# Two mixer layers on one core: a share of the second output projection moves into the attention before it, and four smaller moves

## The chip, the cores and the metric

One Trainium2 chip, one of its cores. The time is device microseconds of one execution: 2440.41 us median of 3 runs (2439.42 to 2441.58). TensorE (PE), VectorE (DVE), ScalarE (ACT), GpSimd (POOL) and SyncE (SP, which issues the transfers) each run their own instruction list in its order; an instruction that waits holds all that stand behind it on its engine.

## The reference

Two layers, run on 1024 latent and 256 context tokens. What matters of a layer:

```
h = rmsnorm(x) * (1 + scale) + shift          # scale, shift, gate from c and w_ada
u = h @ w_in                                   # q, k, v, gates, Hyena, RG-LRU
y_attn = softmax(q k^T / 8) v                  # 8 query heads on 2 key heads, 64 wide
y_hy   = Hyena, a long convolution by FFT;  y_lru = a recurrence in both directions
mix = [y_attn*silu(g_attn), y_hy*silu(g_hy), y_lru*silu(g_lru)]     # 1536 wide
x = x + gate * (mix @ w_out)
```

Latent queries see 512 cached, 1024 latent keys and none of the context; context queries see 256 keys. A last rmsnorm follows layer 2.

## The kernel before, in words

Features lie on partitions, the 1280 tokens along the free axis in chunks of 512, 512 and 256. Each fp32 matrix product is made of three fp16 products: an operand is split into a rounded part (`hi`) and a remainder (`lo = x - hi`), and hi*hi, hi*lo and lo*hi are added up in PSUM.

Stages, in time: **start** (loads; sums of squares of x; scale and shift from `w_ada`; `make_h`, L585), **layer 1**: input projection with recurrence, Hyena and filter spectra woven in (`weave` hands out steps of side generators at fixed rates), **attention 1**, **output projection 1** (with the second layer's filter and `w_ada` work woven in), then **layer 2** in the same way up to **output projection 2**, which runs alone, and the final rmsnorm.

At the start `Squares` squares each x tile on ScalarE and adds the squares up on GpSimd (chunks 1 and 3) or VectorE (chunk 2); TensorE then sums over partitions. Each tile is multiplied by the reciprocal root (half of the tiles on GpSimd), and `make_h` makes the rounded part on ScalarE, the scaled tile on VectorE and the remainder on GpSimd or VectorE. `small_params` (some 60 tiny VectorE operations) stands ahead of this in VectorE's list.

`attention` walks 40 units: 4 pairs of heads, 5 blocks of 256 queries, 2 heads. A unit of latent queries has 12 key tiles in 6 positions of two, one of context queries 1 position. `scores` makes per position 4 score matmuls (L1174, L1175) into one PSUM bank; ScalarE writes exp in fp32 to `by`; the rounded exp is made from the same scores on ScalarE again (`A`), or as a cast on VectorE (`V`) or GpSimd (`G`); the remainder is a subtraction on VectorE or GpSimd. The table `SPLIT` names both engines for each position. `values` multiplies the unit before by v (48 matmuls, L1200 and L1201), VectorE normalises, and after the second head `emit_out` transposes (L1212), gates and splits the result. Between units, row maxima of the next pair are made (`q_maxima`: 48 matmuls of 512 columns, each followed by a VectorE reduction, L1149 and L1150), in bursts of three.

`outproj` (L1291) makes for each of 8 output tiles and 3 chunks 36 matmuls: 12 inputs by three products. Inputs 4 to 11 (Hyena, recurrence) were parked in HBM (`Md`) and are loaded back to `h` tiles; inputs 0 to 3 come from the attention. PSUM is shared by tag: `acc` 3 banks, `s` 2, `m` 2, `o` 1. A scheduler sets each engine's list from the program's order and its estimates.

Of the kernel before, what the change touches and what calls it, by code (L numbers as in the profile page):

```python
# [55 lines left out]
BUFS = {"h": 8, "f": 4, "a": 8, "y": 8, "by": 6, "ld": 4, "bn": 4, "ba": 2, "wr": 4, "wh": 10, "acc": 2, "s": 2, "o": 2, "m": 2}  # L56
# [6 lines left out]
R_FM = (2.006, 1.505)  # L63
# [9 lines left out]
EARLY = (11, 0)  # L73
PTAG = {"acc": "acc", "nacc": 3, "s": "s", "ns": 2, "o": "o", "no": 1, "m": "m", "nm": 2}
BM, VEARLY = 1, True
ORD = "wwwwxwxwxwxwxwxwxwxwcwwww"
# [5 lines left out]
XE = "GVVG"  # L82
SE = "GVG"
# [11 lines left out]
HLO = ((3,), (0,))  # L95
WENG = {"l": "V", "h": "V", "k": "V", "v": "V", "q": "G", "g": "V", "o": "V"}

SPLIT = ("AG", "VV", "AG", "AV", "GG", "AG"), \
    ("VG", "VG", "VV", "VV", "VV", "AG")
# [13 lines left out]
def hybrid_step(ctx, tc, xT, cT, w_ada, w_in, w_out, prm, fpk, w1, w2, w3, decay, ck, cv, wlru,  # L113
# [35 lines left out]
    def stt(out, a, s, b, o0=MUL, o1=ADD, eng=None):  # L149
        (eng or V).scalar_tensor_tensor(out, a, s, b, o0, o1)  # L150
# [44 lines left out]
    Xs = dr.tile([KT, P, T], F32, name="Xs")  # L195
    Qd = dr.tile([2, 2, 2, P, T], F16, name="Qd")
# [264 lines left out]
    def ada():  # L461

        sc = cp.tile([P, KT, 2], F32, name="silu_c")
        th = sm.tile([P, KT, 2], F32, name="th_c")
        act(th, cT_t, AF.Tanh, scale=0.5)
        V.tensor_scalar(th, th, 0.5, 0.5, MUL, ADD)
        tt(sc, th, cT_t, MUL)
        for o in (0, 8):
            p = [PS("s" if o else "acc") for _ in range(2)]
# [78 lines left out]
    class Squares:  # L548
# [17 lines left out]
        def rstd_all(self, chunks):  # L566
            p, t = {}, {}
            for tag, (c0, n) in zip(("m", "m", "acc"), chunks):
                p[c0] = PS(tag)[:, :n]
                PE.matmul(p[c0], ones, self.at(c0, n), start=True, stop=True)  # L570
            for c0, n in chunks:
                t[c0] = rstd_start(p[c0], D)
            for c0, n in chunks:
                rstd_newton(self.at(c0, n), p[c0], D, t[c0])
                yield c0, n, self.at(c0, n)

# [6 lines left out]

    def h_tiles():
        return [S("h", (P, 2, W5), F16) for _ in range(KT)]  # L585

    def make_h(l, h, xs, c0, n):

        s = 0 if c0 < NL else 1
        for i in range(KT):  # L590
            x = xs[i][:, c0:c0 + n]
            hi, lo = h[i][:, 0, c0:c0 + n], h[i][:, 1, c0:c0 + n]
            if l == 0:
                act(hi, x, AF.Identity, scale=sc_t[:, l, i, s:s + 1], bias=sh_t[:, l, i, s:s + 1])
                V.tensor_scalar(x, x, sc_t[:, l, i, s:s + 1], sh_t[:, l, i, s:s + 1], MUL, ADD)
            else:
                act(hi, x, AF.Copy)
            tt(lo, x, hi, SUB, V if i % 4 in HLO[l] else G)

# [15 lines left out]
    class Weights:  # L615


        def __init__(self):
            self.todo, self.done, self.live = [], {}, []
            for l in range(DEPTH):  # L620
                hy = lambda i: [f"hy{n}{i}" for n in (2, 1, 0, 3)]
                names = [f"l{x}{i}" for i in range(4) for x in ("x", "g")]
                names = [n.replace("lg", "gl") for n in names]
                names += hy(0) + hy(1) + ["k", "v", "qa0", "qb0"] + hy(2) + hy(3) + ["qa1", "qb1"]
                names += [f"ga{i}" for i in range(4)] + list(range(KT))
                self.todo += [(l, n) for n in names]
            self.cap = BUFS["wh"]

        def pull(self, need=None):
            while self.todo:  # L630
                l, n = self.todo[0]
                size = 3 if isinstance(n, int) else 2
                if need not in self.done and need is not None:
                    pass
                elif sum(x[1] for x in self.live) + size > self.cap:
                    break
                self.todo.pop(0)
                self.live.append(((l, n), size))
                if isinstance(n, int):
                    v = [split_w(w_out[l, n, :, 512 * i:512 * i + 512], WENG["o"]) for i in (1, 2, 0)]  # L640
                else:
                    v = [split_w(w_in[l, TIDX[n], :, 512 * i:512 * i + 512], WENG[n[0]]) for i in range(2)]
                self.done[l, n] = v
# [487 lines left out]
    def q_maxima(pair, q, tag="m"):  # L1131

        q["q"] = q_head(pair)
        mxl = sm.tile([P, 16, 3], F32, tag="mxl", name=nm("mxl"))
        m = sm.tile([P, 20], F32, tag="mm", name=nm("mm"))
        for i in range(20):
            q_max((*q["q"], mxl, m), i, tag)
            yield
        q["mt"] = q_finish(mxl, m)
        yield  # L1140

    def q_max(st, i, tag="m"):
# [3 lines left out]
        if qt < 8:  # L1146
            for c in range(3):
                p = PS(tag)
                PE.matmul(p, lhs, k1[g][:, 512 * c:512 * c + 512], start=True, stop=True)  # L1149
                V.tensor_reduce(mxl[:, 8 * e + qt, c:c + 1], p, AX.X, MAX)  # L1150
        else:
# [3 lines left out]
            V.tensor_reduce(m[:, o:o + 1], p[:, :NP], AX.X, MAX)  # L1155

# [8 lines left out]
    def scores(st, e, c0, last):  # L1165
# [4 lines left out]
        for s2 in range(0, ns, 2):  # L1170
# [12 lines left out]
            how = SPLIT[last][s2 // 2]  # L1183
# [6 lines left out]
            tt(pt[:, 1, k:k + 2], x, hi, SUB, V if how[1] == "V" else G)  # L1190
        return pts
# [45 lines left out]
    def attention(l, h, st, gates, fill, every):  # L1237
        units = [(p, c0, e) for p in range(4) for c0 in range(0, T, 256) for e in range(2)]
        prev, mix, done = None, [], 0
# [7 lines left out]
        mx, steps = maxima(), 21 * (4 - FM[l])  # L1247
        for n, (pair, c0, e) in enumerate(units):
            k = n % 10
# [4 lines left out]
            if pair < 3:  # L1254
                while done < -(-steps * (n + 1) // 30):
                    next(mx, None)
                    done += 1
                if n == 29:
                    drain(mx)
            pts = scores(st[pair], e, c0, pair == 3)  # L1260
# [7 lines left out]
        drain(fill)  # L1268
        values(*prev[0])
        emit_out(prev[0][4], gates[3], prev[0][2], mix)  # L1270
        return mix

    def outproj(l, mix, xn, sq, rs, ahead):

        for ds in [(d,) for d in range(KT - LAST)] + [tuple(range(KT - LAST, KT))]:
# [4 lines left out]
            for c0, n in CH:  # L1280
                for d in ds:
                    w = W.get(l, d)
                    xi = B("ba")
                    load(xi[:, :n], (xT if l == 0 else Xs)[d, :, c0:c0 + n])
                    acc = PS("acc")
                    for ki in range(NMIX):
                        k = (ki + 4) % NMIX
                        hi, lo = w[ki // 4]
                        cs = slice(P * (k % 4), P * (k % 4) + P)
                        for j, (wt, x) in enumerate(((hi, 0), (hi, 1), (lo, 0))):  # L1290
                            PE.matmul(acc[:, :n], wt[:, cs], mix[k][:, x, c0:c0 + n],  # L1291
                                      start=(ki == 0 and j == 0), stop=(ki == NMIX - 1 and j == 2))
                    if c0 == NL:
                        W.free(l, d)
                    s = 0 if c0 < NL else 1
                    x = xo[d][:, c0:c0 + n]
                    stt(x, acc[:, :n], gt_t[:, l, d, s:s + 1], xi[:, :n])
# [51 lines left out]
    sq, rs = Squares(), {}  # L1349
    for i in range(KT):  # L1350
        for c0, n in CH:
            sq.add(i, xs[i][:, c0:c0 + n], c0, n, ENG[SE[c0 // 512]])
# [7 lines left out]
    for c0, n, r in sq.rstd_all(CH):  # L1360
        for i in range(KT):
            x = xs[i][:, c0:c0 + n]
            tt(x, x, r, MUL, ENG[XE[i % 4]])
    W.pull()
    for l in range(DEPTH):
        h = h_tiles()

        def prep(c0, n):
            if l and c0:
                through(l - 1, c0, n, xs, rs[c0])  # L1370
            make_h(l, h, xs, c0, n)
            if l == 0 and c0 == 0:
                keep_hidden(hid)
            if l == 0 and c0 == NL:
                small_params()
# [36 lines left out]
        mix = attention(l, h, st, gates, fill, EVERY[l])  # L1412
        for i in range(8):
            m = S("h", (P, 2, W5), F16)
            load(m[:, :, :T], Md[i])
            mix.append(m)
# [159 lines left out]
```

## Time and profile before

| | us |
|---|---|
| median of 3 runs | 2440.41 |
| profiled execution | 2441.38 |
| its span, first to last instruction | 2439.6 |
| PE busy | 2123.0 (87%) |
| DVE busy | 1883.6 (77%) |
| ACT busy | 1182.0 (48%) |
| POOL busy | 885.8 (36%) |

The span is the time of the profiled execution but for 1.8 us around it. Busy shares are averages over stages with different limits, so the stages are read one by one. Matmuls are pipelined, and the profile counts each to its own end: a busy PE is not yet a full one.

### The profile page before, as it was taken

What the parts mean: (1) busy time and instruction counts of PE and PEld (TensorE: products, weight loads), DVE (VectorE), ACT (ScalarE), POOL (GpSimd) and SP (SyncE); (2) the same over time, 40 slices, a digit from 0 to 9 for tenths busy, and PEclk for the clock granted to TensorE, in tenths of its full rate; (3) what the DMA queues carried; (4) which work ended last, traced back from release to release, by engine and by line L of the source; (5) the groups of instructions that cost most, each with busy time, mean ns of one, the idle gap of its engine ahead of it and who ended that gap; (6) DMA issues with size and microseconds to landing.
All of it is one profiled execution on the core that took longest, in us unless ns stands there. A gap on an engine that the chain in (4) does not pass through costs nothing. (4 is left out here: it accounts for less than half of the span.)

```text
span 2439.6 us, 37801 instructions
## 1 busy us (share of the span) xinstructions
PE 2123.0 (87%) x14270; PEld 1254.3 (51%) x14270; DVE 1883.6 (77%) x2946; ACT 1182.0 (48%) x2026; POOL 885.8 (36%) x803
## 2 busy tenths in 40 slices
PE   7488878989998878879999898998899888887997
PEld 1144444555455556665445444555555556666554
DVE  7888798387678899986867878747756999998324
ACT  5476655344333556644353676633433346674211
POOL 6732251134213466852111311122341247785100
PEclk8699989999999999979999999999999999998999
DMA  6324215133124400004554122223421431000113
GB/s 260 92 57 123 70 50 134 57 121 123 65 64 151 154 22 7 1 2 125 174 178 149 54 44 42 49 78 114 127 85 60 122 126 54 4 5 1 59 51 108
DMA packets 140871, 205.11 MB, mean 84 GB/s; under 512 B 20612, under 2 KB 68909, under 8 KB 140688
## 3 DMA queue, kind: packets, MB, share of 16 engines
q1 hardware_dynamic: 140688, 202.69, 27.4%
q8 instruction: 112, 1.84, 0.3%
q14 instruction: 71, 0.58, 0.1%
HBM read 160.25 MB, written 38.54 MB: 81 GB/s over the span
## 5 line engine op out<-in xcount | busy, mean ns | idle before, releaser
L659 PE MATMUL acc<-h,wh 128*128 128x512 f16 (+1 forms) x3264 | 861.3, 351 | 48.2 <-ACT h L156 22.4
L659 PE MATMUL acc<-h,wl 128*128 128x512 f16 (+1 forms) x1632 | 572.3, 351 | 0.0
L659 PEld LDWEIGHTS <-wh 128*128 128x128 f16 x3264 | 324.0, 99 | 324.6 <-issue 80.3
L153 POOL TENSOR_TENSOR y<-by,y 128x512 f16<-128x512 f32 x256 | 326.5, 1293 | 147.9 <-ACT y L156 81.7
L659 PEld LDWEIGHTS <-wl 128*128 128x128 f16 x1632 | 162.2, 99 | 156.7 <-issue 29.7
L156 ACT ACTIVATE f<-acc 128x512 f32<-128x512 f32 (+1 forms) x204 | 105.4, 519 | 252.5 <-PE acc L659 243.3
L156 ACT ACTIVATE by<-s 128x512 f32<-128x512 f32 x208 | 126.6, 609 | 160.1 <-PE s L1175 128.7
L1291 PE MATMUL acc<-h,wh 128*128 128x512 f16 (+1 forms) x768 | 202.4, 346 | 0.0
L1150 DVE TENSOR_REDUCE mxl<-m 128x1 f32<-128x512 f32 x288 | 189.0, 680 | 10.1 <-PE m L1149 9.9
L150 DVE SCALAR_TENSOR_TENSOR a<-f,pr,a 128x1024 f32<-128x1024 f32 (+1 forms) x144 | 145.0, 1026 | 59.7 <-ACT a L156 57.5
L1200 PE MATMUL o<-va,y 128*128 128x130 f16 x1600 | 168.3, 228 | 8.9 <-DVE ba L153 5.5
L153 DVE TENSOR_TENSOR y<-by,y 128x512 f16<-128x512 f32 x144 | 169.7, 1210 | 1.0
L1201 PE MATMUL o<-va,y 128*128 128x65 f16 x1600 | 162.8, 199 | 3.8 <-DVE y L153 3.8
L1149 PE MATMUL m<-k,a 128*128 128x512 f16 x288 | 107.4, 395 | 64.3 <-DVE mxl L1150 58.6
L1200 PEld LDWEIGHTS <-y 128*128 128x128 f16 x1600 | 151.2, 102 | 19.9 <-DVE ba L153 8.2
L1291 PEld LDWEIGHTS <-wh 128*128 128x128 f16 x1152 | 111.4, 98 | 96.3 <-issue 14.6
L370 PE MATMUL m<-y,ld 128*128 128x256 f16 x960 | 128.6, 282 | 33.9 <-ACT y L156 14.1
L1201 PEld LDWEIGHTS <-y 128*128 128x128 f16 x1600 | 148.1, 101 | 12.4 <-issue 5.0
L150 DVE SCALAR_TENSOR_TENSOR wl<-wr,wh 128x512 f16<-128x512 f32 x168 | 133.2, 805 | 16.1 <-ACT wh L156 15.1
L156 ACT ACTIVATE wh<-wr 128x512 f16<-128x512 f32 x184 | 112.7, 623 | 59.5 <-PE acc L659 34.6
L153 DVE TENSOR_TENSOR y<-y,y 128x256 f32<-128x256 f32 (+4 forms) x160 | 131.2, 849 | 11.2 <-ACT y L156 11.1
L156 ACT ACTIVATE by<-acc 128x512 f32<-128x512 f32 x192 | 118.2, 615 | 32.4 <-PE acc L1175 25.6
(216 smaller groups left out, 4277.1 us busy)
## 6 DMA issues: line engine op xcount, KB each, us to landing
wr<-in_w_in SPq DMA_DIRECT2D x136, 256.0 KB
bn<-in_w_ada SPq DMA_DIRECT2D x64, 256.0 KB
wr<-in_w_out SPq DMA_DIRECT2D x48, 256.0 KB
ld<-in_fhl SPq DMA_DIRECT2D x56, 192.0 KB
h<-Md SPq DMA_DIRECT2D x16, 640.0 KB
h<-in_w_ada SPq DMA_DIRECT2D x16, 512.0 KB
Md<-ba SPq DMA_DIRECT2D x32, 256.0 KB
Hl<-by SPq DMA_DIRECT2D x32, 256.0 KB
```

Source lines behind the costliest of these rows:

```text
L150: (eng or V).scalar_tensor_tensor(out, a, s, b, o0, o1)
L153: (eng or V).tensor_tensor(out, a, b, op)
L156: A.activation(out, a, f, bias=bias, scale=scale)
L370: PE.matmul(x[:, o], cn[:, y, c], hl[:, z, g], start=(k == 0 and j == 0), stop=(k == 1 and j == 2))
L659: PE.matmul(acc[:, :n], w[k // 4][wi][:, P * (k % 4):P * (k % 4) + P], h[k][:, x, c0:c0 + n], start=(k == 0 and j == 0), stop=(k == KT - 1 ...
L1149: PE.matmul(p, lhs, k1[g][:, 512 * c:512 * c + 512], start=True, stop=True)
L1150: V.tensor_reduce(mxl[:, 8 * e + qt, c:c + 1], p, AX.X, MAX)
L1200: PE.matmul(o[:, qt], p[:, 0], va[g][:, s0 + s], start=(s == 0), stop=False)
L1201: PE.matmul(o[:, qt, 0], p[:, 1], va[g][:, s0 + s, 0], start=False, stop=(s == ns - 1))
L1291: PE.matmul(acc[:, :n], wt[:, cs], mix[k][:, x, c0:c0 + n], start=(ki == 0 and j == 0), stop=(ki == NMIX - 1 and j == 2))
```

## The change

It edits five places.

1. **Start.** `FirstSquares` adds the squares in pairs, and TensorE adds up the pairs over tiles and partitions in PSUM (12 fp32 matmuls in place of 3). The multiplication by the reciprocal root falls into one VectorE operation with the scale; the rounded part gets its shift on ScalarE. Constants load first, and `small_params` is queued behind the third chunk.
2. **Attention, both layers.** The maxima come one at a time after each position, not three at a time; `emit_out` runs one unit later. Rates of the same work ahead of the attention are rescaled to the finer steps.
3. **Attention 2 alone.** `SPLIT` gets a row for each layer: in layer 2 every rounded exp is ScalarE's, 4 of 6 remainders GpSimd's, 2 VectorE's.
4. **Output projection 2.** `soon` makes the products with inputs 4 to 11 inside attention 2, one (output tile, chunk) about every 1.4 units from the fifth on, adds x and stores the sum to HBM (`Xp`); `outproj` loads it and adds inputs 0 to 3.
5. The buffers `ba` grow from 2 to 3.

```diff
-BUFS = {..., "ba": 2, ...}
+BUFS = {..., "ba": 3, ...}
...
+SOON, SOON_RATE, SOON_FROM = (1,), 0.71, 4
-SPLIT = ("AG", "VV", "AG", "AV", "GG", "AG"), \
-    ("VG", "VG", "VV", "VV", "VV", "AG")
+SPLIT = (("AG", "VV", "AG", "AV", "GG", "AG"), ("VG", "VG", "VV", "VV", "VV", "AG")), \
+    (("AG", "AG", "AV", "AG", "AG", "AV"), ("AG", "AG", "AV", "AG", "AG", "AV"))
...
+    class FirstSquares:
+        def add(self, i, x, c0, n):
+            sq = B("bn" if i % 2 else "by")[:, :n]
+            act(sq, x, AF.Square)
+            if i % 2 == 0:
+                self.even[c0] = sq
+            else:
+                tt(sq, sq, self.even[c0], ADD, G if c0 == 512 else V)
+                PE.matmul(self.acc[c0][:, :n], ones, sq, start=(i == 1), stop=(i == KT - 1))
...
     def make_h(...)
-            if l == 0:
-                act(hi, x, AF.Identity, scale=sc_t[:, l, i, s:s + 1], bias=sh_t[:, l, i, s:s + 1])
-                V.tensor_scalar(x, x, sc_t[:, l, i, s:s + 1], sh_t[:, l, i, s:s + 1], MUL, ADD)
+            if r is not None:
+                sh = sh_t[:, l, i, s:s + 1]
+                done = stt(x, x, sc_t[:, l, i, s:s + 1], r, MUL, MUL)
+                act(hi, x, AF.Identity, bias=sh)
+                if i in HFIRST:
+                    stt(lo, x, sh, hi, ADD, SUB)
+                else:
+                    act(x, x, AF.Identity, bias=sh)
+                    tt(lo, x, hi, SUB, G)
...
     def attention(...)
+            if sooner and n >= SOON_FROM:
+                have += SOON_RATE
+                if have >= 1.0:
+                    have -= 1.0
+                    next(sooner, None)
...
                 values(*prev[0])
+                if late:
+                    emit_out(*late.pop())
                 if prev[0][1]:
-                    emit_out(prev[0][4], gates[prev[1]], prev[0][2], mix)
+                    late.append((prev[0][4], gates[prev[1]], prev[0][2], mix))
...
+    def soon(l, parked):
+        for d in range(KT):
+            w = W.get(l, f"u{d}")
+            for c0, n in CH:
+                xi = B("ld")[:, :n]
+                load(xi, (xT if l == 0 else Xs)[d, :, c0:c0 + n])
+                acc = out_acc(w, [None] * 4 + parked, range(4, NMIX), c0, n)
+                if c0 == NL:
+                    W.free(l, f"u{d}")
+                s = 0 if c0 < NL else 1
+                stt(xi, acc, gt_t[:, l, d, s:s + 1], xi)
+                load(Xp[d, :, c0:c0 + n], xi)
+                yield
...
-        for c0, n, r in sq.rstd_all(CH):
-            x = xs[i][:, c0:c0 + n]
-            tt(x, x, r, MUL, ENG[XE[i % 4]])
+    first = sq.rstd()
...
+                with tc.issue_after(done.ins):
+                    small_params()
```

TensorE's list in attention 2, where a unit's transposes stand. Before (L1174 and L1175 are scores, L1149 a maximum, L1212 the transposes):

```order
L1174 LDWEIGHTS k_88
L1174 MATMUL acc_22599<-a_20764,k_88 128x256
L1149 LDWEIGHTS a_21917
L1149 MATMUL m_22561<-k_88,a_21917 128x512
L1212 MATMUL o_22546<-ident,ba_22237 128x128 x2
L1175 LDWEIGHTS k_90
L1175 MATMUL acc_22599<-a_21908,k_90 128x256
```

Now (L1228 and L1229 are the values, L1321 the early output products, L1240 the transposes):

```order
L1228 MATMUL o_23145<-va_93,y_22951 128x130
L1229 LDWEIGHTS y_22951
L1229 MATMUL o_23145<-va_93,y_22951 128x65
L1321 LDWEIGHTS wh_20753
L1321 MATMUL acc_23207<-h_19632,wh_20753 128x512
...
L1321 MATMUL acc_23207<-h_19634,wh_20753 128x512
L1240 MATMUL o_23199<-ident,ba_22676 128x128 x2
L1321 LDWEIGHTS wl_20754
L1321 MATMUL acc_23207<-h_19634,wl_20754 128x512
```

The transposes moved from between the scores to between the early output products; a group of 24 of these stands whole behind a unit's 48 value matmuls, in 24 places.

VectorE's list in attention 2, about one unit. Before (L1187 is a cast to the rounded exp, `y` from `by` a remainder, L1150 a maximum):

```order
L1187 CAST y_20807<-by_20817 128x512
L153 TENSOR_TENSOR ba_20662<-ba_20662,ri_20869 128x2x64
L153 TENSOR_TENSOR y_20807<-by_20817,y_20807 128x512
L150 SCALAR_TENSOR_TENSOR f_18729<-o_20874,f_18729 128x256
L1150 TENSOR_REDUCE mxl_20773<-m_20880 128x1
L153 TENSOR_TENSOR y_20826<-by_20836,y_20826 128x512
```

Now (L1175 is a maximum, `ld` from `acc` the end of an early output product, `wl` a weight's remainder):

```order
L1175 TENSOR_REDUCE mxl_20918<-m_21722 128x1
L154 TENSOR_TENSOR y_21705<-by_21706,y_21705 128x512
L1175 TENSOR_REDUCE mxl_20918<-m_21725 128x1
L154 TENSOR_TENSOR y_21733<-by_21746,y_21733 128x512
L1232 RECIPROCAL ri_21802<-o_21753 128x2
L151 SCALAR_TENSOR_TENSOR f_18985<-o_21807,f_18985 128x256
L151 SCALAR_TENSOR_TENSOR wl_21843<-wr_21840,wh_21842 128x512
L151 SCALAR_TENSOR_TENSOR ld_21813<-acc_21815,gt_t,ld_21813 128x256
```

The casts are gone, and each third and sixth position's remainder, and the ends of the early products, stand in line with the maxima.

## Rows read from the trace of the kernel before

**Rows 1.** Windows by stage: us, busy us of each engine (instructions), granted clock, DMA.

```profile
0.00:130.00 130.00, 81.89 (x238) 27.32 (x239) 109.23 (x210) 69.64 (x119) 85.77 (x77) 0.79 0.47 166
...
821.00:1108.00 287.00, 230.33 (x2596) 178.32 (x2595) 265.71 (x477) 168.73 (x333) 195.55 (x174) 0.92 0.11 34
...
1362.00:1987.00 625.00, 574.12 (x3214) 319.54 (x3212) 461.26 (x645) 300.70 (x475) 156.38 (x175) 0.97 0.27 76
1987.00:2271.00 284.00, 231.86 (x2609) 181.82 (x2607) 267.48 (x480) 169.88 (x337) 202.91 (x177) 0.92 0.12 37
2271.00:2426.60 155.60, 155.31 (x861) 83.79 (x857) 48.80 (x79) 26.50 (x45) 0.67 (x1) 1.00 0.21 63
2426.60:2440.00 13.40, 0.70 (x2) 0.30 (x2) 9.06 (x16) 1.76 (x4) 2.69 (x3) 0.64 0.65 232
```

**Rows 2.** Groups by line, DVE in output projection 2: count, busy us, mean ns, idle.

```profile
L150 DVE SCALAR_TENSOR_TENSOR wl<-wr,wh 128x512 f16<-128x512 f32 x14 | 9.7, 690 | 3.6 <-ACT wh L156 2.9 <-DMA ba<-Xs 0.5
L150 DVE SCALAR_TENSOR_TENSOR f<-acc,gt_t,ba 128x512 f32<-128x512 f32 x8 | 6.0, 751 | 45.6 <-PE acc L1291 39.4 <-issue 6.3
```

**Rows 3.** Timeline of PE in one unit of attention 2: start us, us.

```profile
2041.25 0.38 PE L1149 MATMUL m<-k,a 128*128 128x512 f16 x1
2041.47 0.27 PE L1174 MATMUL acc<-a,k 128*128 128x256 f16 x1
2041.58 0.27 PE L1175 MATMUL acc<-a,k 65*128 65x256 f16 x1
2041.69 0.22 PE L1200 MATMUL o<-va,y 128*128 128x130 f16 x1
...
2043.78 0.38 PE L1149 MATMUL m<-k,a 128*128 128x512 f16 x1
```

**Rows 4.** Groups by line, DVE in attention 2.

```profile
L1150 DVE TENSOR_REDUCE mxl<-m 128x1 f32<-128x512 f32 x144 | 94.0, 679 | 3.0 <-PE m L1149 3.0
L153 DVE TENSOR_TENSOR y<-by,y 128x512 f16<-128x512 f32 x72 | 86.2, 1228 | 0.5
L1187 DVE CAST y<-by 128x512 f16<-128x512 f32 x66 | 45.8, 713 | 4.1 <-ACT by L156 3.6
```

**Rows 5.** One tile's operations, `y` on DVE in attention 2: min, median, max ns.

```profile
L153 DVE TENSOR_TENSOR y<-by,y x72: 677/1154/1700, 1997.6 to 2262.2; 128x512 f16<-128x512 f32 x72
```

**Rows 6.** Groups by line, ACT in attention 2.

```profile
L156 ACT ACTIVATE by<-s 128x512 f32<-128x512 f32 x104 | 63.2, 609 | 81.7 <-PE s L1175 62.4 <-issue 10.0 <-POOL y L153 9.0
...
L156 ACT ACTIVATE y<-acc 128x512 f16<-128x512 f32 x56 | 35.4, 632 | 0.0
```

**Rows 7.** Groups by line, POOL in attention 2.

```profile
L153 POOL TENSOR_TENSOR y<-by,y 128x512 f16<-128x512 f32 x128 | 164.7, 1304 | 63.0 <-ACT y L156 31.4 <-DVE y L1187 26.8 <-issue 2.4
L1189 POOL TENSOR_SCALAR y<-by 128x512 f16<-128x512 f32 x24 | 17.4, 726 | 5.5 <-ACT by L156 5.5
```

**Rows 8.** Timeline of POOL in the start; in brackets idle before and its end.

```profile
70.13 12.43 POOL L153 TENSOR_TENSOR f<-f,by 128x512 f32<-128x512 f32 x2 [16.65 <-DVE by L150]
```

**Rows 9.** Timeline of DVE in the start.

```profile
51.60 1.22 DVE L216 TENSOR_SCALAR fin_t<-pr 128x8 f32<-128x8 f32 x1
...
60.05 0.17 DVE L241 TENSOR_SCALAR lr_sp<-z 128x8 f32<-128x8 f32 x1
```

**Rows 10.** Timeline of PE in the start.

```profile
82.24 1.01 PE L659 MATMUL acc<-h,wh 128*128 128x512 f16 x2 [16.23 <-ACT h L156]
...
96.97 0.59 PE L659 MATMUL acc<-h,wh 128*128 128x512 f16 x1 [5.02 <-POOL h L153]
```

**Rows 11.** Timeline of ACT in the start.

```profile
115.92 0.60 ACT L156 ACTIVATE f<-acc 128x512 f32<-128x512 f32 x1 [5.63 <-POOL h L153]
```

**Rows 12.** Groups by line, PE in the start.

```profile
L570 PE MATMUL m<-by,ones 128*128 128x512 f32 x4 | 3.8, 1101 | 0.0
```

**Rows 13.** Waits in attention 1: engine, line, waited for: us, times, longest.

```profile
PE m L1149 <- DVE mxl L1150: 31.8, 29, 3.1
...
PE o L1212 <- DVE ba L153: 14.0, 11, 3.9
```

More of the change, by code (lines that the diff above doesn't have):

```diff
@@ L81 @@
 XL = "V"
-XE = "GVVG"
-SE = "GVG"
 CE = "V"
@@ L195, in hybrid_step @@
     Xs = dr.tile([KT, P, T], F32, name="Xs")
+    Xp = dr.tile([KT, P, T], F32, name="Xp")
     Qd = dr.tile([2, 2, 2, P, T], F16, name="Qd")
@@ L468, in ada @@
         for o in (0, 8):
-            p = [PS("s" if o else "acc") for _ in range(2)]
+            p = [PS("m" if o else "s") for _ in range(2)]
             for k in range(KT):
@@ L564, in add @@
                 tt(d, d, sq, ADD, eng)
[L566 to L575, printed above, removed]
         def rstd(self, c0, n):
@@ L624, in __init__ @@
                 names += hy(0) + hy(1) + ["k", "v", "qa0", "qb0"] + hy(2) + hy(3) + ["qa1", "qb1"]
-                names += [f"ga{i}" for i in range(4)] + list(range(KT))
+                names += [f"ga{i}" for i in range(4)]
+                names += [f"{x}{d}" for x in "ur" for d in range(KT)] if l in SOON else list(range(KT))
                 self.todo += [(l, n) for n in names]
@@ L640, in pull @@
                     v = [split_w(w_out[l, n, :, 512 * i:512 * i + 512], WENG["o"]) for i in (1, 2, 0)]
+                elif n[0] in "ur":
+                    v = [split_w(w_out[l, int(n[1]), :, 512 * i:512 * i + 512], WENG["o"])
+                         for i in ((1, 2) if n[0] == "u" else (0,))]
                 else:
@@ L1136, in q_maxima @@
         for i in range(20):
-            q_max((*q["q"], mxl, m), i, tag)
-            yield
+            yield from q_max((*q["q"], mxl, m), i, tag)
         q["mt"] = q_finish(mxl, m)
@@ L1163, in q_finish, with scores @@
         return mt
-    def scores(st, e, c0, last):
+    def scores(l, st, e, c0, last, tick):
         g, q1, q2 = st
@@ L1182, in scores @@
             act(x, p, AF.Exp, scale=0.125)
-            how = SPLIT[last][s2 // 2]
+            how = SPLIT[l][last][s2 // 2]
             if how[0] == "A":
@@ L1235, in gate_steps, with attention @@
             yield from inproj_steps(l, f"ga{i}", h, gated(gates[i]))
-    def attention(l, h, st, gates, fill, every):
+    def attention(l, h, st, gates, fill, every, sooner=None):
         units = [(p, c0, e) for p in range(4) for c0 in range(0, T, 256) for e in range(2)]
-        prev, mix, done = None, [], 0
+        prev, mix, have, late = None, [], 0.0, []
         def maxima():
@@ L1245, in maxima, with tick @@
                 st[p] = (*q["q"], q_rest(p, q["mt"]))
-        mx, steps = maxima(), 21 * (4 - FM[l])
+        mx, rate, due = maxima(), 53 * (4 - FM[l]) / 150, [0.0]
+        def tick():
+            due[0] += rate
+            while due[0] >= 1.0:
+                due[0] -= 1.0
+                next(mx, None)
         for n, (pair, c0, e) in enumerate(units):
-            k = n % 10
             if n % every == 0:
                 next(fill, None)
+            if sooner and n >= SOON_FROM:
[3 more added lines that the diff above has]
+                    next(sooner, None)
             if n == 4 and FM[l] > 1:
                 st[1] = (*q_head(1), q_rest(1, st[1]))
[L1254 to L1260, printed above, removed]
+            while pair not in st:
+                next(mx)
+            pts = scores(l, st[pair], e, c0, pair == 3, tick if pair < 3 else lambda: None)
             if e == 0:
@@ L1264, in attention, with out_acc @@
                 values(*prev[0])
+                if late:
+                    emit_out(*late.pop())
                 if prev[0][1]:
-                    emit_out(prev[0][4], gates[prev[1]], prev[0][2], mix)
+                    late.append((prev[0][4], gates[prev[1]], prev[0][2], mix))
             prev = ((st[pair], e, c0, pts, ob), pair)
         drain(fill)
+        if sooner:
+            drain(sooner)
         values(*prev[0])
+        for x in late:
+            emit_out(*x)
         emit_out(prev[0][4], gates[3], prev[0][2], mix)
         return mix
+    def out_acc(w, mix, ks, c0, n):
+        acc = PS("acc")
+        for i, k in enumerate(ks):
+            hi, lo = w[i // 4]
+            cs = slice(P * (k % 4), P * (k % 4) + P)
+            for j, (wt, x) in enumerate(((hi, 0), (hi, 1), (lo, 0))):
+                PE.matmul(acc[:, :n], wt[:, cs], mix[k][:, x, c0:c0 + n],
+                          start=(i == 0 and j == 0), stop=(i == len(ks) - 1 and j == 2))
+        return acc[:, :n]
+    def soon(l, parked):
+        for d in range(KT):
+            w = W.get(l, f"u{d}")
+            for c0, n in CH:
+                xi = B("ld")[:, :n]
[6 more added lines that the diff above has]
+                load(Xp[d, :, c0:c0 + n], xi)
+                yield
     def outproj(l, mix, xn, sq, rs, ahead):
@@ L1281, in outproj @@
                 for d in ds:
[L1282 to L1292, printed above, removed]
+                    name = f"r{d}" if l in SOON else d
+                    w = W.get(l, name)
+                    xi = B("ld" if l in SOON else "ba")[:, :n]
+                    load(xi, (Xp if l in SOON else xT if l == 0 else Xs)[d, :, c0:c0 + n])
+                    acc = out_acc(w, mix, range(4) if l in SOON else [*range(4, NMIX), *range(4)], c0, n)
                     if c0 == NL:
-                        W.free(l, d)
+                        W.free(l, name)
                     s = 0 if c0 < NL else 1
                     x = xo[d][:, c0:c0 + n]
-                    stt(x, acc[:, :n], gt_t[:, l, d, s:s + 1], xi[:, :n])
+                    stt(x, acc, gt_t[:, l, d, s:s + 1], xi)
                     sq.add(d, x, c0, n, V)
@@ L1370, in prep @@
                 through(l - 1, c0, n, xs, rs[c0])
-            make_h(l, h, xs, c0, n)
+            done = make_h(l, h, xs, c0, n, first[c0] if l == 0 else None)
             if l == 0 and c0 == 0:
@@ L1411, in hybrid_step, with fetch @@
         fill = chain(gate_steps(l, h, gates, range(N_G[l], 4)))
[L1412 to L1416, printed above, removed]
+        parked = []
+        def fetch():
+            for i in range(8):
+                m = S("h", (P, 2, W5), F16)
+                load(m[:, :, :T], Md[i])
+                parked.append(m)
+        if l in SOON:
+            drain(fill)
+            fetch()
+            mix = attention(l, h, st, gates, fill, EVERY[l], soon(l, parked))
+        else:
+            mix = attention(l, h, st, gates, fill, EVERY[l])
+            fetch()
+            mix += parked
         xs, sq, rs = [], Squares(), {}
```

35 lines of the change are left out of this document (23 added, 12 removed).

## Prediction

> **What bounds the kernel now.** I read the windows by stage first [rows 1]. The reader is to see that each stage has its own limit. In layer 2 TensorE is busy 574.12 of 625 us (92%), in output projection 2 155.31 of 155.6 at a granted clock of 1.00: there it is full, nothing else works much, and the time is its count of matmuls. In attention 2 VectorE is busy 267.48 of 284 us (94%), TensorE 231.86, GpSimd 202.91, ScalarE 169.88. In the start VectorE has 109.23 of 130, TensorE 81.89 at a clock of 0.79.
>
> The next view tells how much of attention 2 TensorE really needs. In the timeline of one unit [rows 3] a 512-column matmul lasts 0.38 us, but the next starts 0.22 after it; a 256-column one follows after 0.11; the 48 value matmuls go from 2041.69 to 2043.78, 2.09 us. Attention 2 has 800 score matmuls of 256 columns (88 us by 0.11), 144 maxima (31.7 by 0.22), the values of 32 large units (48 each) and 8 small ones (8 each), 1600 matmuls (69.7 by 2.09/48): 189 us, 191 with the transposes. So about 93 of its 284 us are free on TensorE. The Trainium skill ("Perfetto Trace Analysis", Identifying the Most-Contended Engine) says that matmul busy time is a bad measure of nearness to the limit since matmuls are pipelined. Spacing against duration agrees; by busy shares only 52 us would be free and the stage below could not be under 336 us, by spacing 295.
>
> **The change part by part.** The sums are made against the profiled execution, 2441.38 us, 0.97 above the median of the runs.
>
> *Early products and the new split (attention 2 and output projection 2 together, now 439.6 us).* Inputs 4 to 11 are 8 of 12, so 576 of 864 matmuls leave output projection 2: two thirds of 155.6 is 103.7, and 51.9 stay. TensorE's own work in attention 2 becomes 191 + 104 = 295 us. That is the lower end if nothing waits; at the 92% of layer 2 it would be 321. The upper end is 284 + 104 = 388, nothing hidden.
>
> Which of the two it is nearer to depends on the other engines. VectorE loses 66 casts (45.8) and 8 of 72 remainders (8 x 1.23 = 9.8) [rows 4]; it gains 24 ends of early products, like those of the second row of output projection 2 (16 x 0.75 + 8 x 0.48, the half-wide taken as somewhat over half) and 16 remainders of weights (0.69) [rows 2]: 267.5 - 55.6 + 26.9 = 239. A remainder takes 0.68 to 1.70 us [rows 5]; were the 64 left all at 1.70, VectorE would have 270. ScalarE takes over 90 rounded exps at 0.63 (57) and rounds 16 weights (10): 170 + 67 = 237 [rows 6]. GpSimd loses 24 casts (17.4) and gains 8 subtractions of 1.30: 196 [rows 7]. All four are then under 295: no engine but TensorE is full. The casts' wait for the fp32 exp and GpSimd's 26.8 us of waiting for casts go; late next is ScalarE, behind scores.
>
> Per large unit: TensorE has 24 scores (2.64), some 4.5 maxima (1.0) and its part of the transposes, 4.0 in all, values 2.09, and in 24 units or so an early group of 24 matmuls, 24 x 0.216 = 5.2 (0.216 being 155.3 over 576 wide and 288 half-wide matmuls) or 2.6. That makes 11.3, 8.7 or, without one, 6.1. ScalarE's twelve exps are 12 x 0.62 = 7.4, and the bank behind the last needs VectorE's remainder or normalising, 1.2: 8.6. The larger rules a unit. In pairs 0 to 2 13 units at 11.3, 4 at 8.7, 7 at 8.6 make 242, six small units at 4.7 28; pair 3, without maxima, 82. Together 352. Some of ScalarE's lag in units without a group is caught up in the next, so I take 345. With the 51.9 that is 396.9: **-43** (bounds -93, or -67 at the 92%, to 0).
>
> The early products also issue 24 loads of x, 24 stores, 16 weight tiles again and 24 loads in the last stage, all on queues that move little: DMA is busy 0.12 of attention 2 and 0.21 of the last stage [rows 1]; they are hidden unless a load stands behind a store that waits for VectorE. I cost them at nothing; uncovered, one wait of a microsecond or two in each of 24 groups.
>
> *Start.* What ended the waits is a chain. GpSimd's first two products by the reciprocal root took 12.43 us [rows 8], all the while VectorE made its own; the first dense matmul stood 16.23 us for `h` [rows 10], and the first evacuation waited 5.63 us for GpSimd's remainder [rows 11]. The change takes the products from GpSimd altogether, and three of eight remainders. Gain: 12.4 + 5.6 = 18. `small_params` (51.60 to 60.22, 8.6 us) [rows 9] moves behind the third chunk; its work comes back where layer 1's VectorE waits, so if it too is won the gain is 26.7. Against it stand nine more matmuls by `ones`, 0.95 each [rows 12], 8.6 us on an idle TensorE, and a VectorE that keeps about its work. I take **-18**, range 0 to -27.
>
> *Later transposes and single maxima, attention 1.* TensorE waits 31.8 us for reductions in front of a maximum and 14.0 us for `ba` in front of the transposes [rows 13]. Both are taken out of bursts. But VectorE has 265.71 of 287 us [rows 1] and the same operations as before, so at most its 21.3 idle us can go. I take a third, **-7**; -14 if all of the transposes' wait goes, +4 if a reduction now holds one position more (the longest wait was 3.9). That `emit_out` is a unit later is what the third `ba` is for; what stands behind it is output projection 1, which has other inputs first. The rescaled rates hand out the same work: nothing.
>
> Sum: -43 - 18 - 7 = -68; 2441.4 - 68 = **2373**.
>
> **The rivals.**
>
> *A: only the attention gains.* In the start VectorE's work is conserved, so the shorter chain ends in its queue, and attention 1 stays with VectorE. For it: 109.2 of 130 busy. Against: the 16.23 and 12.43 of rows that name GpSimd. 2441.4 - 43 = 2398.
>
> *B: the early products are not hidden.* If TensorE's free 93 us are waits within chains (exp, remainder, values) that no other matmul can fill, because the group stands whole in its list behind the values, attention 2 takes 388. With 51.9 that is 440, and 18 + 7 remain: 2416. For it: in-order lists, and groups of 24 in one piece. Against: ScalarE and GpSimd work on in the meantime on what the scores left.
>
> *C, slower: ScalarE comes in series.* A bank of scores is now held through two exps of ScalarE, and the early product takes one of three `acc` banks, of which the scores also live. If scores then move at ScalarE's pace and the values and the early group come only after, a unit costs 7.4 + 1.2 + 2.09 + 3.2 (the early groups' 104 over 32) = 13.9: 32 x 13.9 + 37.6 for the small ones = 482, + 51.9 = 534, so +95; less 25, +70: 2511. It decides from a mean large unit of (439.6 + 25 - 51.9 - 37.6)/32 = 11.7 us on; below, the whole is faster. For it: ScalarE rises from 170 to 237, and it already waits 62.4 us for scores [rows 6]. Against it: the order puts 48 values and 24 early products, 7.3 us, behind all 24 scores, in which time ScalarE works off the banks it has.
>
> **How the numbers follow.** Forecast 0.75, its own range 2342 to 2400; A 0.08; B 0.10; C 0.07. Faster and slower here mean by over 0.2% (4.9 us), what a measurement of this kernel tells from nothing. Forecast, A and most of B are faster: 0.89. C is slower, with one part in ten of B, 0.08; 0.03 lies between. The 80% range leaves out C and the deepest corner (attention 2 at TensorE's 295 with the start's full 27 would be 2316): 2333 to 2418, so that A and B are in it.
>
> **What would show it.** Right: attention 2 of about 345 us, with TensorE over 85% busy, VectorE near 70%, ScalarE near 68%; output projection 2 near 52; the first dense matmul at 64 to 70 and the first evacuation near 98; attention 1 near 280 with the wait for `ba` mostly gone. Wrong: attention 2 above 390 with TensorE waiting for ScalarE or for a bank (B above 385, C above 430); a first dense matmul still near 80 (A); or an output projection 2 well above 52, if the loads of `Xp` come late.

## The result and the profile after

The changed kernel takes 2385.81 us (median; 2383.06 to 2389.05), the kernel before, beside it on the same chip, 2440.99: a ratio of 0.9775 (0.9758 to 0.9792), 55 us less. 2373 was predicted, with a range of 2333 to 2418.

The windows by stage of the changed kernel (columns as in [rows 1]; start, rest of layer 1, attention 1, output projection 1, layer 2, attention 2 to its last transposes, output projection 2, and what follows TensorE's last product):

```profile
0.00:130.00 130.00, 102.66 (x361) 39.77 (x362) 107.82 (x222) 90.39 (x161) 56.86 (x54) 0.93 0.53 181
130.00:811.00 681.00, 593.55 (x3339) 333.73 (x3339) 522.94 (x740) 316.30 (x495) 197.28 (x170) 0.95 0.32 90
811.00:1095.00 284.00, 232.19 (x2621) 181.58 (x2619) 259.35 (x482) 167.29 (x334) 200.46 (x177) 0.93 0.12 37
1095.00:1348.80 253.80, 236.83 (x1297) 118.62 (x1297) 182.46 (x279) 113.97 (x194) 39.24 (x23) 0.98 0.49 154
1348.80:1972.50 623.70, 573.53 (x3211) 319.23 (x3209) 461.60 (x643) 299.11 (x474) 158.00 (x175) 0.97 0.28 78
1972.50:2315.10 342.60, 319.56 (x3209) 228.05 (x3207) 233.23 (x452) 220.40 (x443) 179.95 (x161) 0.99 0.22 68
2315.10:2362.40 47.30, 46.90 (x258) 25.15 (x257) 25.43 (x42) 14.82 (x26) 0.67 (x1) 1.00 0.32 87
2362.40:2386.00 23.60, 2.60 (x7) 0.80 (x4) 19.30 (x33) 4.08 (x8) 2.83 (x3) 0.58 0.61 223
```

With the same cuts between stages (the last product or the last transposes of each) in the trace of before, the span's 53.7 us are: to the end of layer 1's products 10.0 less (820.9 to 810.9), attention 1 5.2 less (289.4 to 284.2), output projection 1 2.0 more, layer 2 0.7 less, attention 2 and output projection 2 together 49.9 less (439.8 to 389.9), and the tail 10.2 more (13.3 to 23.5). In attention 2 VectorE went from 94% to 68% busy, TensorE from 82% to 93%.

The tail is VectorE's. It is busy for 19.30 of 23.60 us, almost all of it the last norm of all three chunks. In the kernel before, the norm of the first chunk and the start of the second's ran beside output products, two thirds of which now stand in attention 2 (VectorE's tail was 9.06 busy of 13.40 in [rows 1]).

### The profile page after: what moved, and what is told of

The parts are those of the page before. It is cut to its first block, busy times and chain, and to the rows that moved or that the text cites. A ratio compares the mean times of both kernels' runs of the same rounds, so it can differ in the third digit from the quotient of the medians.

```text
span 2385.9 us, 38028 instructions
## 1 busy us (share of the span) xinstructions
PE 2107.8 (88%) x14288; PEld 1246.9 (52%) x14288; DVE 1812.1 (76%) x2888; ACT 1226.4 (51%) x2132; POOL 835.3 (35%) x762
## 5 line engine op out<-in xcount | busy, mean ns | idle before, releaser
L685 PE MATMUL acc<-h,wl 128*128 128x512 f16 (+1 forms) x1632 | 572.5, 351 | 0.0
L154 POOL TENSOR_TENSOR y<-by,y 128x512 f16<-128x512 f32 x264 | 319.7, 1227 | 211.1 <-issue 93.7
L1321 PE MATMUL acc<-h,wh 128*128 128x512 f16 (+1 forms) x768 | 203.6, 348 | 0.0
L1175 DVE TENSOR_REDUCE mxl<-m 128x1 f32<-128x512 f32 x288 | 188.0, 680 | 7.2 <-PE m L1174 7.0
L1228 PE MATMUL o<-va,y 128*128 128x130 f16 x1600 | 166.8, 224 | 2.0 <-DVE f L151 1.6
L1229 PE MATMUL o<-va,y 128*128 128x65 f16 x1600 | 161.6, 195 | 5.1 <-POOL y L154 4.7
L154 DVE TENSOR_TENSOR y<-by,y 128x512 f16<-128x512 f32 x136 | 137.1, 1017 | 34.6 <-ACT y L157 34.2
L1229 PEld LDWEIGHTS <-y 128*128 128x128 f16 x1600 | 144.7, 99 | 34.0 <-issue 18.4
L1321 PEld LDWEIGHTS <-wh 128*128 128x128 f16 x1152 | 109.7, 98 | 95.0 <-issue 19.5
L1228 PEld LDWEIGHTS <-y 128*128 128x128 f16 x1600 | 146.6, 99 | 21.0 <-issue 14.4
L1174 PE MATMUL m<-k,a 128*128 128x512 f16 x288 | 110.7, 387 | 37.3 <-DVE mxl L1175 35.8
L154 DVE TENSOR_TENSOR y<-y,y 128x256 f32<-128x256 f32 (+4 forms) x160 | 129.8, 841 | 13.8 <-ACT y L157 13.7
L151 DVE SCALAR_TENSOR_TENSOR wl<-wr,wh 128x512 f16<-128x512 f32 x168 | 129.8, 785 | 11.4 <-ACT wh L157 10.4
L1321 PE MATMUL acc<-h,wl 128*128 128x512 f16 (+1 forms) x384 | 133.6, 348 | 0.0
```

The lines of the kernel that those rows point to most:

```text
L151: return (eng or V).scalar_tensor_tensor(out, a, s, b, o0, o1)
L154: (eng or V).tensor_tensor(out, a, b, op)
L685: PE.matmul(acc[:, :n], w[k // 4][wi][:, P * (k % 4):P * (k % 4) + P], h[k][:, x, c0:c0 + n], start=(k == 0 and j == 0), stop=(k == KT - 1 ...
L1228: PE.matmul(o[:, qt], p[:, 0], va[g][:, s0 + s], start=(s == 0), stop=False)
L1229: PE.matmul(o[:, qt, 0], p[:, 1], va[g][:, s0 + s, 0], start=False, stop=(s == ns - 1))
L1321: PE.matmul(acc[:, :n], wt[:, cs], mix[k][:, x, c0:c0 + n], start=(i == 0 and j == 0), stop=(i == len(ks) - 1 and j == 2))
```

## The experiments

Each ratio is to runs of the kernel before on the same chip. For attention 2 the traces give one more number, worked out from the timeline of TensorE: the time by which a matmul starts later than the columns of the one ahead of it take at full clock (0.22 us for 512 [rows 3]), where that is over 0.15 us. It is called TensorE's standing time below. It is counted to the last transposes; some of the expectations counted a shorter window, and so a few us less. The stages repeat well: four kernels with the changed kernel's attention 2 (the changed one, experiments 9, 10 and 11) take 342.6 or 342.7 us there.

**1. No early products.**

```
-SOON = (1,)
+SOON = ()
```

> The changed kernel with all products of output projection 2 left in output projection 2; the new split, start, maxima and transposes stay. Theory (the early products fill time in which TensorE waits): attention 2 can't fall much below ScalarE's 235 us of work plus its waits, 250 to 265, output projection 2 is back at 156 and the tail behind its last matmul back at 13; together 419 to 434 where the changed kernel has 413, so 2392 to 2407. Rival (the split made the gain, by taking VectorE's load away, and the products only changed places): attention 2 falls to 235 or less and the total is 2386 or lower.

The kernel took 2401.72 us, ratio 0.9853 (0.9827 to 0.9878), within the theory's bounds. But theory and rival were both half right. Attention 2 fell to 256.2 us, 30 under the kernel before, with the split, the maxima and the transposes alone (experiment 4 will give the split 27 of the 30):

```profile
1980.50:2236.60 256.10, 224.00 (x2625) 172.03 (x2623) 209.12 (x411) 208.77 (x427) 183.46 (x161) 0.98 0.13 42
```

Of the 30 us, 19 are standing time (67 before, 48 here). The other 11 lie in smaller gaps and in the granted clock, 0.92 before [rows 1] and 0.98 here: with its two levels, 2.4 and 1.2 GHz, an estimate from these means is 45 us at the lower one before and 10 here. No run changes the clock alone, so its part is not told apart.

Output projection 2 is back at 152.7 us and the tail at 13.5. The early products then make attention 2 86.5 us longer, output projection 2 105.4 shorter, the tail 10 longer: a gain of 9 us by these stages, 16 by the medians. The rest lies ahead of attention 2, where the two kernels are the same.

**2. The early products alone**, on the kernel before.

```
 kernel before
+SOON = (1,); soon(), out_acc(), Xp
```

> The kernel before with the early products alone: old start, old split in both layers, maxima in threes, transposes at once, two ba buffers. Theory: TensorE's free 93 us take most of the 104 us even so, VectorE has 267 + 27 = 294 us of work in some 345: 2406 to 2421. Rival (only the relieved VectorE lets the products in): attention 2 grows by the whole 104 us, 2436 to 2446.

The kernel took 2423.34 us, ratio 0.9948 (0.9928 to 0.9969): 13 us less, between theory and rival. Attention 2 took 364.9 us, so 79 of some 104 us of early products were not hidden; standing time is 52, where the kernel before has 67.

**3 and 4. Layer 1's split in layer 2**, with and without the early products.

```
-SPLIT[1] = ("AG", "AG", "AV", "AG", "AG", "AV") x2
+SPLIT[1] = SPLIT[0]
```

> The changed kernel with layer 1's split in layer 2 too. Theory: VectorE gets 55 us back, some 285 us in an attention 2 of 331: it is near the bound, attention 2 gets 5 to 15 us longer, 2391 to 2401. Rival (the split carries the gain): 25 us or more, 2411 and up.

> The changed kernel without early products and with layer 1's split in layer 2. Without early products but with the new split attention 2 took 256.2 us to its last transposes (before: 286.0), with both 342.7, with the early products but the old split 378.6. Theory (each of the two takes from the same free time of TensorE, so the split is worth more where the early products stand behind it): attention 2 goes to 278 to 286 us here, the total to 2423 to 2432, so the split is worth 22 to 30 us without the early products, 36 with them. Rival (they add up): 36 us also here, 2436 to 2440.

With the early products the kernel took 2422.32 us, ratio 0.9941 (0.9918 to 0.9964): the split carries 36 us, the rival's case. Without them it took 2421.91, ratio 0.9921 (0.9899 to 0.9943): there the split is worth 20, a little under the theory's 22 to 30 and far from the rival's 36. The two edits do not add up; with the old split, early products in whole groups bring nothing that these runs show. Their stages:

| split, early products | attention 2 | standing time | output projection 2 | tail |
|---|---|---|---|---|
| before (old, none) | 286.0 | 67 | 153.8 | 13.3 |
| old, none | 283.0 | 69 | 153.3 | 13.3 |
| old, whole groups | 378.6 | 67 | 48.5 | 23.5 |
| new, none | 256.2 | 48 | 152.7 | 13.5 |
| new, whole groups (changed) | 342.7 | 33 | 47.3 | 23.5 |

Attention 2 less TensorE's standing time is 208 to 219 us without early products and 310 to 312 with them. So with the old split they filled next to none of the standing time, though VectorE was not full either:

```profile
1967.60:2346.20 378.60, 330.22 (x3200) 233.44 (x3198) 286.63 (x525) 177.92 (x352) 203.88 (x177) 0.96 0.20 61
```

The waits of that kernel in attention 2 (engine and its tile, then what it waited for: us, times, longest) show who stands besides:

```profile
ACT by L157 <- PE s L1202: 110.1, 30, 8.2
...
DVE ld L151 <- PE acc L1321: 59.6, 16, 6.1
...
PE m L1174 <- DVE mxl L1175: 21.3, 34, 2.2
```

While TensorE runs a group of 24 in one piece, ScalarE and VectorE run dry (up to 8.2 and 6.1 us at a time; without early products ScalarE waits 61.1 us in place of 110.1, at most 4.7 at a time). Afterwards TensorE waits for VectorE as before: of its 67 us, 35 stand in front of a maximum, 14 in front of transposes and 3 in front of a score, against 33, 19 and 3 without early products. ScalarE's timeline of that kernel shows such a wait (TensorE's group runs from 2107.8 to some 2113):

```profile
2105.41 0.68 ACT L157 ACTIVATE y<-acc 128x512 f16<-128x512 f32 x1
2113.67 0.60 ACT L157 ACTIVATE by<-s 128x512 f32<-128x512 f32 x1 [7.58 <-PE s L1202]
```

Whole groups are not always hidden as badly. Experiment 2 has the same split and groups, but maxima in threes and transposes at once, and its attention 2 is 14 us shorter; with the new split they take the standing time from 48 to 33.

**5 and 6. Groups of 12 between the scores**, with the new and with the old split.

```
-    acc = out_acc(w, [None] * 4 + parked, range(4, NMIX), c0, n)
-    ...
-    stt(xi, acc, gt, xi); load(Xp[...], xi); yield
+    for k0 in (4, 8):
+        acc = out_acc(w[(k0 - 4) // 4:], ..., range(k0, k0 + 4), c0, n)
+        stt(xi, acc, gt, xi)
+        if k0 == 8: load(Xp[...], xi)
+        yield                     # asked for in tick(), 0.273 a position
```

> The changed kernel with each group of 24 early matmuls made in two groups of 12, asked for after a position of the scores and no longer once at a unit's start, so that they stand between scores on TensorE; VectorE gets 24 more ends (some 16 us). In the changed kernel TensorE still stands 32 us in attention 2 (47 without the early products, 63 with them and the old split), and ScalarE waits 75 us for scores, mostly while a whole group runs. Theory (a group in one piece behind the values fills no wait, it moves it): pieces between the scores take 10 to 25 of the 32 us, 2361 to 2376. Rival (what is left is TensorE's wait for VectorE's reductions in front of maxima, and more ends on VectorE add to it): 2383 to 2395.

> The kernel with groups of 12 between the scores, and layer 1's split in layer 2. With whole groups and this split attention 2 took 378.6 us to its last transposes, 95.6 more than without early products (283.0): of some 104 us nearly nothing hidden, though TensorE waited 63 us and VectorE was busy for only 277 of 365. Theory (a whole group makes VectorE and ScalarE wait for TensorE, and afterwards TensorE for them; pieces let them work on): 15 to 35 us less, 2387 to 2407. Rival (VectorE, with 12 us more of ends, sets the pace by the casts and remainders between two scores, whatever stands between): 2415 to 2430.

With the old split the kernel took 2390.10 us, ratio 0.9811 (0.9794 to 0.9828), 32 less than with whole groups and within the theory's bounds: attention 2 fell from 378.6 to 344.5, the standing time from 67 to 35 (in front of maxima from 35 to 18, of transposes from 14 to 5), although VectorE has more to do:

```profile
1971.30:2315.80 344.50, 320.12 (x3195) 228.32 (x3193) 290.16 (x549) 180.81 (x352) 203.79 (x177) 0.98 0.21 67
```

and its waits there:

```profile
ACT by L157 <- PE s L1202: 84.8, 40, 8.8
...
DVE ld L151 <- PE acc L1322: 16.5, 19, 2.1
```

VectorE's wait for the early sums fell from 59.6 to 16.5 us. That the same products fill half of the standing time in pieces between the scores, and next to none of it whole between the units, shows what hid them badly: how they were cut and placed, not their amount. The edit changes the size of a group and its place at once; which of the two does it is not shown. With the new split the step is smaller, as less was left: 2378.96 us, ratio 0.9757 (0.9738 to 0.9777), over the theory's 2361 to 2376 and under the rival's case, with attention 2 down from 342.7 to 330.8 and standing time from 33 to 23. By the runs alone that ratio can't be told from the changed kernel's; its trace, 11.9 us shorter in just this stage, can (experiment 12 has 330.8 there too).

**7. Transposes at once.**

```
-    if late: emit_out(*late.pop())
-    if last head: late.append(...)
+    if last head: emit_out(...)
```

> The changed kernel with the transposes straight behind the unit's second values, as before. Theory: the wait for ba in front of them (14.0 us in attention 1 before) comes back for the part that the next wait does not hide: 3 to 5 us in each attention, 2390 to 2396. Rival (waits in front of the maxima take its place, or, behind a group of early products, VectorE has long normalised): 2383 to 2388.

The kernel took 2390.15 us, ratio 0.9789 (0.9769 to 0.9810), 4 us above the changed kernel's and within the error of the two. The time lies in the theory's range, but not for its reason: both attentions are as long as the changed kernel's or shorter (281.7 and 342.0), so the 4 us are not from there.

**8. Maxima in threes.**

```
-    tick()                            # one maximum after each position
...
+    while done < -(-steps * (n + 1) // 30): next(mx, None); done += 1
```

> The changed kernel with the maxima in threes between the units and their rates as before. Theory: TensorE waits again for VectorE's reductions, 31.8 us where the single ones in attention 1 wait 26.4, and some 10 us more in attention 2: 2389 to 2398. Rival (with old split and early products the threes and transposes at once had an attention 2 of 364.9 us, single and late 378.6): the threes are as good or better, 2374 to 2386.

The maxima ahead of the attention are in threes here too, at the rates of before. The kernel took 2384.26 us, ratio 0.9767 (0.9751 to 0.9784): the rival's case. Attention 1 takes 283.3 us, attention 2 339.4, against 284.2 and 342.7: one at a time gains nothing here.

**9 and 10. The start before, and `small_params` at its head.**

```
-FirstSquares; stt(x, x, sc, r, MUL, MUL); act(hi, x, bias=sh); ...
+Squares, rstd_all, products on GpSimd and VectorE, as before
```

```
-    with tc.issue_after(done.ins):
-        small_params()
+    small_params()
```

> The changed kernel with the start of the kernel before. The trace shows the first dense matmul 14.8 us earlier, the lead at 2% of layer 1's products 24 us and from 40% on 10. Theory (VectorE, full from 60 to 120 us, and its side work in layer 1 take the rest back): the whole costs 10 us, 2394 to 2398. Rival (the lead lost in layer 1 is lost to something else of the change, and the start alone would be worth its 18 to 24 us): 2403 to 2410.

> The changed kernel with small_params no longer held behind the third chunk: its some 60 tiny operations go back to the front of VectorE's list. Theory (VectorE has the same work up to 200 us either way, 170 us in both kernels, and the lead of the first products is spent on it later): the lead at 2% of layer 1's products falls from 24 by about 8 us, layer 1 ends as before to within 4 us, 2382 to 2390. Rival (the order of the start is worth what it shows at the first matmul): 2391 to 2396.

With the old start the kernel took 2391.84 us, ratio 0.9816 (0.9794 to 0.9837): the new start is worth 10 us by the ratios, 6 by the medians, 5 by the profiled spans, so 5 to 10, at or under the theory's 10 and far from the rival's 18 to 24. With `small_params` first it took 2388.07, ratio 0.9786 (0.9770 to 0.9801), no difference that can be told. Its lead over the kernel before is 22.2 us at 2% of layer 1's products (the changed kernel's is 24.3; a fall of 8 was expected), 12.1 at 10% and 7.6 at 20% (19.6 and 13.7), and the same at 30% (10.6 and 10.4). So what the start wins early is not what arrives. The changed kernel's own rows show the early part:

```profile
67.45 1.01 PE L685 MATMUL acc<-h,wh 128*128 128x512 f16 x2 [3.65 <-ACT h L157]
```

```profile
97.42 0.60 ACT L157 ACTIVATE f<-acc 128x512 f32<-128x512 f32 x1 [0.60 <-POOL h L154]
```

The first dense matmul stands 3.65 us for `h`, not 16.23 [rows 10], and the first evacuation comes 18.5 us earlier than in [rows 11]. That VectorE takes the lead back is likely, as it is busy 170 of the first 200 us in both kernels, but no run takes work off it there, so it is not shown.

**11. The tail.**

```
-for ds in [(d,) for d in range(6)] + [(6, 7)]:
+for ds in [(d,) for d in range(2)] + [(2, ..., 7)]:      # layer 2
```

> The changed kernel with the last 6 instead of 2 output tiles of layer 2 walked chunk by chunk together, so that the first chunk's sum of squares is done 24 us before TensorE ends, not 8. Behind the last matmul the changed kernel has 23.5 us, the kernel before 13.3; VectorE fills them with the last norm of all chunks. Theory (the norm of the first two chunks had been hidden behind matmuls that are now in attention 2): the tail falls to 14 to 16, the total to 2376 to 2379. Rival (VectorE has 50 us of work in the last 82 us and is the bound of the whole of output projection 2): it is late anyway, 2383 to 2387.

The kernel took 2381.99 us, ratio 0.9758 (0.9730 to 0.9786); the tail fell from 23.5 to 16.4 us, output projection 2 grew from 47.3 to 49.0. That is the theory's mechanism with a little less of it than the 14 to 16 us expected; the 4 us of the runs lie between theory and rival and are within their error.

**12. Groups of 12, and all 8 tiles by chunk.**

> The same with all 8 output tiles of layer 2 walked chunk by chunk. Theory (the tail falls from 23.5 us to some 13 and nothing else changes): 8 to 10 us under the kernel with halves alone. Rival (VectorE's 50 us in the last 80 are the bound): within 3 us of it; with 6 tiles the tail was 16.4 us and the time 4 us less.

The kernel took 2372.49 us (2370.92 to 2377.85), ratio 0.9728 (0.9711 to 0.9745): 13 us under the changed kernel, the intervals apart, and the best version here. Against groups of 12 alone it is 6.5 us by the medians, where the theory said 8 to 10, and those two intervals overlap. The trace shows both edits: attention 2 takes 330.8 us, and the tail is 14.5 with half the work on VectorE that the changed kernel's had.

```profile
2304.50:2354.60 50.10, 49.97 (x274) 26.88 (x273) 34.95 (x57) 16.76 (x29) 0.67 (x1) 1.00 0.44 132
2354.60:2369.10 14.50, 1.54 (x5) 0.54 (x3) 10.23 (x19) 2.18 (x5) 2.69 (x3) 0.58 0.55 199
```

## Why the prediction was right, and where it was not

*Attention 2 and output projection 2* (forecast -43, measured -49.9, and -39.7 with the tail). The length was met: 345 forecast, 342.7 measured, with VectorE at 68% and ScalarE at 64%. That it was met so closely is in part luck, because the reason given was met only in part. I let the early products fill the 93 us that I counted as free on TensorE. Standing time was 67; the rest of the 93 was the low clock (0.92 [rows 1]; 0.98 to 0.99 after) and small gaps. Of the gain, 30 us are the shorter attention 2 that experiment 1 has without any early product, and 19 are the early products' (105.4 out, 86.5 in), of which the tail took 10 back.

The step that failed is the unit without a group, priced at 8.6 us by twelve exps of 0.62 one after another and a wait of 1.2. Counted from a unit's last value matmul to the next one's, large units of pairs 0 to 2 take 7.05 us in experiment 1 (mean of 23) and 7.5 in the changed kernel where they have no group (mean of 8); with a whole group they take 10.7 there, where 11.3 was forecast. The kernel before made its large units in 7.8, so its own trace spoke against 8.6. Nor had the sum a term for the start of the stage: the first unit's values end 19 us in, some 11 more than a unit takes. The exps overlap as matmuls do; I read starts for TensorE and durations for ScalarE. The changed kernel's timeline of ScalarE shows 0.48 from start to start:

```profile
2103.00 0.58 ACT L157 ACTIVATE by<-acc 128x512 f32<-128x512 f32 x1
2103.48 0.59 ACT L157 ACTIVATE y<-acc 128x512 f16<-128x512 f32 x1
2103.95 0.60 ACT L157 ACTIVATE by<-s 128x512 f32<-128x512 f32 x1
2104.43 0.61 ACT L157 ACTIVATE y<-s 128x512 f16<-128x512 f32 x1
```

By starts, twelve exps are 5.8 us, under TensorE's own 6.1 for a unit without a group; so most of what a group adds makes the stage longer (86.5 of some 104 us). The errors cancelled: too little gain for the split, too much for the hiding.

*Rival B* was nearer to the mechanism than its chance of 0.10 says: with the old split (experiment 3) its price nearly came true, 378.6 us for a forecast 388, and experiment 6 fits the reason it gave, the group in one piece. It did not decide because the new split shortened the stage by itself. *Rival C* did not occur: in the changed kernel's attention 2 ScalarE waits 75 us for TensorE, and TensorE's waits for ScalarE add up to under 3.

```profile
ACT by L157 <- PE s L1202: 74.8, 23, 6.7
```

*Output projection 2*: 51.9 forecast, 47.3 measured; 34 of its 288 matmuls run ahead of the last transposes, where the cut lies. *The tail* was missing from the sum: nothing forecast, +10.2 measured. I asked for each edit what hides it, but not what the moved products had hidden: much of the last norm of two chunks on VectorE.

*Start* (forecast -18, measured -10.0 at layer 1's end, 5 to 10 by the runs). First matmul and first evacuation came where they were forecast (67.45 in 64 to 70; 97.42 near 98). The failed step is that a lead at the first evacuation lasts: of 24.3 us at 2% of layer 1's products 10 are left at 30%. Rival A's reason, VectorE's queue, fits that and is not shown. How much of the 10 us is the start's is open: with the old start but single maxima and three `ba` buffers (experiment 9) layer 1 ended 7.8 us before the kernel before without any early lead, with the new start but maxima in threes (experiment 8) 13.1 us before it, and kernels with the same code up to there end layer 1 between 807 and 816 us.

*Attention 1* (forecast -7, measured -5.2, and 2.0 given back in output projection 1). No gain of the change is shown there. Neither of the two edits that I priced shows alone (experiments 7 and 8), and the kernel of experiment 2, which has attention 1 as it was, takes 282.9 us for it, 6.5 less than the kernel before with the same instructions in the same order on all four engines:

```profile
820.90:1110.30 289.40, 232.73 (x2614) 179.56 (x2613) 267.30 (x483) 168.73 (x333) 195.88 (x174) 0.92 0.11 34
820.50:1103.40 282.90, 228.96 (x2615) 178.98 (x2613) 264.30 (x483) 168.12 (x334) 197.97 (x174) 0.93 0.11 35
```

The first line is the kernel before, the second experiment 2. All kernels but the one before take 282 to 285 us there, so the 5.2 us are most likely a matter of that one trace; that the forecast of -7 came close is luck.

## What to carry to other kernels

Work moved into an engine's waits hides best cut into pieces and placed inside the chain that makes the waits; in one piece it stopped here the engines that were to end those waits, and with the old split the waits came back behind it. Ask of moved work not only what hides it but also what it was hiding. Read start-to-start spacing on every engine before its durations are added up, and check the price of a unit against the units of the trace at hand. Before a gain of a few us is put down to an edit, look how much a stage with the same instructions differs from trace to trace.

## What the runs showed of the hardware

ScalarE's exps of 128x512 from PSUM start 0.48 us apart while their recorded durations in one row of twelve rise from 0.60 to 0.72 us, so a sum of durations overstates ScalarE by a quarter or more. The first, second and last of that row, in the changed kernel:

```profile
2122.29 0.60 ACT L157 ACTIVATE by<-s 128x512 f32<-128x512 f32 x1
2122.78 0.59 ACT L157 ACTIVATE y<-s 128x512 f16<-128x512 f32 x1
...
2127.55 0.72 ACT L157 ACTIVATE y<-acc 128x512 f16<-128x512 f32 x1
```

Of the two GpSimd products that took 12.43 us at the start [rows 8] the first alone took 11.2 us and the second 1.26. The first began 0.4 us before VectorE's own products and ended 1.7 us after the last of them:

```profile
70.57 1.29 DVE L153 TENSOR_TENSOR f<-f,by 128x512 f32<-128x512 f32 x2
...
78.87 0.75 DVE L153 TENSOR_TENSOR a<-a,by 128x256 f32<-128x256 f32 x2
```

The other GpSimd operations of this shape in the start took 1.3 to 1.8 us, and the traces of experiments 2 and 9, with the same start, show the 11.2 us and the 1.7 again. In the changed kernel, where VectorE makes all of these products as SCALAR_TENSOR_TENSOR, GpSimd's remainders of 128x512 beside a full VectorE take 3.35 us for two. What makes the difference no run isolates.

```profile
70.94 3.35 POOL L154 TENSOR_TENSOR h<-f,h 128x512 f16<-128x512 f32 x2 [20.82 <-ACT f L157]
```
